# Differential scores over stacked halves, and wide matmuls for the neighbourhood heads' q and k

## The chip, the core and the metric

The kernel runs on one core of a Trainium2 chip, as one launch. The metric is the device time of a launch in microseconds (us), from start to end; lower is better. The engines named below are PE (matrix), ACT (scalar), DVE (vector), POOL (GpSimd) and SP, whose queue issues the transfers. Each works through its own list of instructions in order, and they wait for each other by semaphores.

## The reference

Two layers of an encoder over 256 tokens of width 2048, all in float32. What matters here, shortened:

```python
h = rmsnorm(x, attn_norm[l])
qd, kd, vd, qn, kn, vn = split(h @ w_in[l])        # six blocks of 1024 columns
qd, kd = rope(qd), rope(kd)                        # 8 heads x 2 maps x 64
# differential heads (8, v of 128 columns)
p = softmax(q @ k.T * 64**-0.5)                    # one for each of the two maps
o = rmsnorm((p[0] - lam * p[1]) @ v, subln_g) * (1 - lambda_init)
# neighbourhood heads (8, of 128 columns), a window in the 64-wide grid
p = softmax(q @ k.T * 128**-0.5 + bias)
o_na = rmsnorm(p @ v over all heads, na_norm[l])
x = x + concat(o, o_na) @ w_out[l]
u = relu(rmsnorm(x, mlp_norm[l]) @ w_mlp_in[l])    # 8192 wide
x = x + (u * u) @ w_mlp_out[l]
```

## The kernel before

**Split products.** A float32 operand is cut into a high and a low part (`fp32r`), and a product is three matmuls: high by high, low by high, high by low. The weights stream from HBM as slabs of 128 x 2048 (`raw`, three buffers). For each half of a slab ACT copies the high part (`whi`, line 130) and DVE subtracts to get the low part (`wlo`, line 131), with four buffers of each, so two slabs are ready ahead.

**The shapes of a product.** `block_product` (lines 140 to 171) has the activations stationary and 512 columns of weights moving; it fills two PSUM tiles of the tag `acc`, which has four buffers. It makes the q, k and v of the differential heads, v of the neighbourhood heads, and the output products. `stationary_product` has the weights stationary: for each of 16 slices three matmuls of 256 columns (lines 180 to 182), into one `acc` tile; it makes q and k of one neighbourhood head from one slab each. `wide_product` (lines 185 to 202) does the MLP's first product: the high and low activations stand side by side, so 16 matmuls of 512 columns do two of the three parts (line 192) and 16 of 256 columns the third (line 196). Its two halves are then added: ACT copies one out of PSUM (`low`), and DVE adds the other to it (`whole`, a tile of the tag `o` with four buffers).

**A layer.** Differential heads come in two blocks of four. For a block, `to_sbuf_rope` rotates q and k, transposes them and splits them into two `qkT` tiles each. `diff_head` makes the scores of both maps, each over 64 partitions (lines 362 to 364), takes exponents on ACT, combines the two maps on DVE (`wd`), transposes `wd` (line 315), copies it on ACT (`wT`), multiplies by v (line 326), squares the result on ACT (`junk`), takes the norm on POOL (`comb`), scales on DVE (`o`, line 334, tag `o`), transposes again (line 337) and splits into `mix`. Then, twice, v for four neighbourhood heads (`vs`) and four times `na_head`: q and k, scores (lines 405 to 407), exponents, a division by the sum on DVE (line 423), transposes, the split of these into `half` tiles, and three matmuls by v (lines 429 to 431). Output product and MLP follow.

**What sets the order.** A scheduler lays out each engine's list before the run. A tile waits for a free buffer of its tag. `acc` has four: v of the neighbourhood heads holds two until it is in `vs`, and each q or k holds one until it is out of PSUM.

Of the kernel before, what the change touches and what calls it, by code (L numbers as in the profile page):

```python
# [11 lines left out]
F32 = mybir.dt.float32  # L12
F32R = mybir.dt.float32r
# [5 lines left out]
P = 128  # L19
D = 2048  # L20
S = 256
# [27 lines left out]
def body(ctx, tc, x, x_t, w, gains_in, gains_o, final_g, lam_in, rpb, ident_in, rope_in, mask_in, out):  # L49
# [120 lines left out]
                one(k, t)  # L170
        return acc

    def stationary_product(h_t):

        parts = next_slab()
        acc = ps.tile([P, S], F32, name="accu", tag="acc", bufs=4)
        for k in range(NK):
            hi, lo = parts[k // 8]
            wh, wl = hi[:, (k % 8) * P:(k % 8 + 1) * P], lo[:, (k % 8) * P:(k % 8 + 1) * P]
            nc.tensor.matmul(acc, wh, h_t[k][:, 0], start=k == 0, stop=False)  # L180
            nc.tensor.matmul(acc, wh, h_t[k][:, 1], start=False, stop=False)  # L181
            nc.tensor.matmul(acc, wl, h_t[k][:, 0], start=False, stop=k == NK - 1)  # L182
        return acc

    def wide_product(h_t):


# [62 lines left out]

    def to_sbuf_rope(acc, r, which):

        dst = [act.tile([P, 4, S], F32R, name="qkT", tag="A", bufs=12) for _ in range(2)]
        for t in range(NT):
            nat = work.tile([P, NB], F32, name="nat", tag="nat", bufs=3)
            tmp = work.tile([P, NB], F32, name="tmp", tag="tmp", bufs=2)
            a3 = acc[t].rearrange("p (g d) -> p g d", d=QKD)
            n3, t3 = nat.rearrange("p (g d) -> p g d", d=QKD), tmp.rearrange("p (g d) -> p g d", d=QKD)
            G, H2 = NB // QKD, QKD // 2
            cos, sin = rope[:, t, 2 * which, :], rope[:, t, 2 * which + 1, :]  # L260
            nc.vector.scalar_tensor_tensor(n3, a3, r[t], cos[:, None, :].to_broadcast([P, G, QKD]),
                                           op0=ALU.mult, op1=ALU.mult)
            nc.vector.scalar_tensor_tensor(t3[:, :, :H2], a3[:, :, H2:], r[t],
                                           sin[:, None, :H2].to_broadcast([P, G, H2]),
                                           op0=ALU.mult, op1=ALU.mult)
            nc.vector.scalar_tensor_tensor(t3[:, :, H2:], a3[:, :, :H2], r[t],
                                           sin[:, None, H2:].to_broadcast([P, G, H2]),
                                           op0=ALU.mult, op1=ALU.mult)
            nc.gpsimd.tensor_tensor(nat, nat, tmp, op=ALU.add)
            transpose_heads(dst, nat, t)  # L270
        return dst

    def transpose_heads(dst, nat, t):
        pt = ps.tile([P, 4, P], F32, name="tp", tag="tp", bufs=2)
        for j in range(4):
            nc.tensor.transpose(pt[:, j, :], nat[:, j * P:(j + 1) * P], ident)  # L276
        hi, lo = (part[:, :, t * P:(t + 1) * P] for part in dst)
        nc.scalar.activation(hi, pt, AF.Copy)
        nc.vector.tensor_sub(lo, pt, hi.bitcast(F32))

    def to_sbuf_v(acc, r):
        v = act.tile([P, NT, NB], F32, name="v", tag="A", bufs=12)
        for t in range(NT):
            nc.scalar.activation(v[:, t, :], acc[t], AF.Copy, scale=r[t])
        return v

    def to_sbuf_v_split(acc, r):
        v = [act.tile([P, NT, NB], F32R, name="vs", tag="A", bufs=12) for _ in range(2)]
        for t in range(NT):
            split(v[0][:, t, :], v[1][:, t, :], acc[t], r[t])  # L290
        return v
# [48 lines left out]
    def split_mix(src, gain):  # L340
        m, mix_half[0] = mix_half[0], None
        i = 1
        if m is None:
            m = act.tile([P, 2, 2, S], F32R, name="mix", tag="A", bufs=12)
            mix_half[0] = m
            i = 0
        split(m[:, i, 0], m[:, i, 1], src, gain)
        return m[:, i]
# [3 lines left out]
    def diff_head(q, k, v, j, nlam, gsub):  # L352
        neg = small.tile([P, 2, NT], F32, name="neg")
        sm = small.tile([P, 2, NT], F32, name="sm")
        pr = []
        sc = [ps.tile([P, NT, S], F32, name="sc", tag="sc", bufs=2) for _ in range(2)]
        for t in range(NT):
            for m in range(2):
                rows = slice(m * QKD, (m + 1) * QKD)
                qh, ql = (part[rows, j, t * P:(t + 1) * P] for part in q)  # L360
                kh, kl = (part[rows, j, :] for part in k)
                nc.tensor.matmul(sc[m][:, t, :], qh, kh, start=True, stop=False)  # L362
                nc.tensor.matmul(sc[m][:, t, :], ql, kh, start=False, stop=False)  # L363
                nc.tensor.matmul(sc[m][:, t, :], qh, kl, start=False, stop=True)  # L364
        for m in range(2):
            nc.vector.tensor_reduce(neg[:, m, :], sc[m], axis=AX.X, op=ALU.max, negate=True)
            p = work.tile([P, NT, S], F32, name="pr", tag="pr", bufs=3)
            for t in range(NT):
                nc.scalar.activation(p[:, t, :], sc[m][:, t, :], AF.Exp, bias=neg[:, m, t:t + 1],
                                     accum_out=sm[:, m, t:t + 1])  # L370
            pr.append(p)
        rs = small.tile([P, 2, NT], F32, name="rs")
        nc.vector.reciprocal(rs, sm)
        c = small.tile([P, NT], F32, name="c")
        nc.vector.scalar_tensor_tensor(c, sm[:, 0, :], nlam, rs[:, 1, :], op0=ALU.mult, op1=ALU.mult)
        wd = work.tile([P, NT, S], F32, name="wd", tag="wd")
        for t in range(NT):
            nc.vector.scalar_tensor_tensor(wd[:, t, :], pr[1][:, t, :], c[:, t:t + 1], pr[0][:, t, :],
                                           op0=ALU.mult, op1=ALU.add)
        po = weights_times_v(wd, v, j)  # L380
        ss = small.tile([P, NT], F32, name="sso")
        for t in range(NT):
            junk = work.tile([P, HD], F32, name="junk", tag="junk", bufs=1)
            nc.scalar.activation(junk, po[:, t, :], AF.Square, scale=rs[:, 0, t:t + 1],
                                 accum_out=ss[:, t:t + 1])
        r = rms_scale(ss, NT, HD)
        comb = small.tile([P, NT], F32, name="comb")
        nc.gpsimd.tensor_tensor(comb, r, rs[:, 0, :], op=ALU.mult)
        return to_mix(po, comb, gsub)

    def na_head(h, h_t, v, rq, rb, table, gain, sq_sum):
        q = split_plain(stationary_product(h_t), [P, S], "half", 8)
        acc = stationary_product(h_t)
        kr = work.tile([P, S], F32, name="kr", tag="nat", bufs=3)
        nc.vector.tensor_mul(kr, acc, rb)
        k = split_plain(kr, [P, S], "half", 8)
        bias = work.tile([P, 6, GRID_W], F32, name="bias", tag="bias")
        th = table[:, h, :]
# [21 lines left out]
        rs = small.tile([P, NT], F32, name="rs")  # L420
        nc.vector.reciprocal(rs, sm)
        for t in range(NT):
            nc.vector.tensor_scalar(pr[:, t, :], pr[:, t, :], rs[:, t:t + 1], None, op0=ALU.mult)
        wt = split_plain(transposed_weights(pr), [P, NT, S], "wT", 3)
        po = ps.tile([P, S], F32, name="tp", tag="tp", bufs=2)
        j = h % 4
# [23 lines left out]

    def prologue(s):

        st = act.tile([P, 4, S], F32, name="xT", tag="A", bufs=12)

        def load(k0, k1):
            stream(st[:, k0:k1], x_t[s, :, k0:k1])
            for k in range(k0, k1):
                norm.store(4 * s + k, st[:, k, :])

        if s == 0:  # L460
            load(0, 2)
            x_rest[0] = lambda: load(2, 4)
        else:
            load(0, 4)

    for l in range(DEPTH):
# [62 lines left out]
        h_t = norm.h_t  # L529
        last = l == DEPTH - 1  # L530
        if last:
            gb = [act.tile([P, HALF], F32, name="gb", tag="A", bufs=12) for _ in range(2)]
            for i, g in enumerate(gb):
                nc.scalar.dma_start(g, bass.AP(tensor=final_g.tensor, offset=final_g.offset + i * HALF,
                                               ap=[[0, P], [1, HALF]]))
            xg = []
        nxt = Norm(2 * l + 2) if not last else Norm(0)
        for c in range(N_CHUNK):
            us = []
            for f in range(F_PER_CHUNK):  # L540
                u = wide_product(h_t)
                u2 = work.tile([P, S], F32, name="u2", tag="o", bufs=4)
                nc.vector.scalar_tensor_tensor(u2, u, 0.0, u, op0=ALU.max, op1=ALU.mult)
                if f % 2 == 0:
                    pair = act.tile([P, 2, 2, S], F32R, name="u2T", tag="A", bufs=12)
                split(pair[:, f % 2, 0], pair[:, f % 2, 1], u2, 1.0)
                us.append(pair[:, f % 2])
            for n in range(4):
# [113 lines left out]
```

## Time and profile before

| What | Value |
|---|---|
| device time, median of 3 runs | 2237.27 us (2236.66 to 2237.89) |
| device time of the profiled execution | 2237.57 us |
| its span, first to last instruction | 2235.7 us |
| PE busy | 2220.2 us (99%) |
| DVE busy | 1349.1 us (60%) |
| ACT busy | 1076.5 us (48%) |
| PE clock, mean granted share | 0.999 |

Matmuls are pipelined, and a new one starts before the last has ended. So what a matmul costs is the distance from its start to the next start, and not its own duration; this distance is read in the timelines.

### The profile page before, as it was taken

What the parts mean: (1) busy time and instruction counts of PE and PEld (TensorE: products, weight loads), DVE (VectorE), ACT (ScalarE), POOL (GpSimd) and SP (SyncE); (2) the same over time, 40 slices, a digit from 0 to 9 for tenths busy, and PEclk for the clock granted to TensorE, in tenths of its full rate; (3) what the DMA queues carried; (4) which work ended last, traced back from release to release, by engine and by line L of the source; (5) the groups of instructions that cost most, each with busy time, mean ns of one, the idle gap of its engine ahead of it and who ended that gap; (6) DMA issues with size and microseconds to landing.
All of it is one profiled execution on the core that took longest, in us unless ns stands there. A gap on an engine that the chain in (4) does not pass through costs nothing.

```text
span 2235.7 us, 29767 instructions
## 1 busy us (share of the span) xinstructions
PE 2220.2 (99%) x11856; PEld 1910.4 (85%) x11856; DVE 1349.1 (60%) x1743; ACT 1076.5 (48%) x1579; POOL 91.6 (4%) x136
## 2 busy tenths in 40 slices
PE   8999999999999999999999999999999999999998
PEld 7889998888888888888888899988888888888886
DVE  6657665664565565565566566666655655655654
ACT  6546544554453454454445564445434534544543
POOL 1111000000000000000010111000000000000000
PEclk9999999999999999999999999999999999999999
DMA  9443445555555555555654434554555555555553
GB/s 329 151 181 140 170 161 180 187 188 190 198 191 193 188 189 188 198 188 186 200 186 164 171 136 170 188 187 177 186 200 192 189 188 193 190 192 197 188 188 132
DMA packets 61291, 414.38 MB, mean 185 GB/s; under 512 B 7008, under 2 KB 9184, under 8 KB 11872
## 3 DMA queue, kind: packets, MB, share of 16 engines
q1 hardware_dynamic: 60720, 411.40, 51.4%
q8 instruction: 93, 1.52, 0.3%
q10 hardware_dynamic: 432, 1.08, 0.1%
q14 instruction: 46, 0.38, 0.0%
HBM read 410.35 MB, written 2.10 MB: 184 GB/s over the span
## 4 chain that ended last, share of the span: by engine, by line
PE 99%; DMA 1%; DVE 0%; ACT 0%; POOL 0%; issue 0%; ACTq 0%; POOLq 0%
PE accw L192 21%; PE acc L155 18%; PE acc L153 18%; PE acc L154 18%; PE accw L196 11%; PE accu L180 3%; PE accu L182 3%; PE accu L181 3%; PE tp L326 1%; PE tp L315 1%; PE tp L240 0%; DMA raw<-in_w 0%; PE sc L362 0%; PE tp L276 0%; PE sc L364 0%; PE sc L363 0%
## 5 line engine op out<-in xcount | busy, mean ns | idle before, releaser
L131 DVE TENSOR_TENSOR wlo<-raw,whi 128x1024 fp32r<-128x1024 f32 (+1 forms) x770 | 934.7, 1228 | 632.3 <-ACT whi L130 504.7
L130 ACT ACTIVATE whi<-raw 128x1024 fp32r<-128x1024 f32 (+1 forms) x770 | 814.2, 1058 | 905.1 <-PE acc L154 565.2
L192 PE MATMUL accw<-hT,whi 128*128 128x512 f32 x2048 | 491.2, 391 | 0.0
L192 PEld LDWEIGHTS accw<-hT,whi 128*128 128x128 f32 x2048 | 376.1, 188 | 72.8
L154 PE MATMUL acc<-whi,u2T 128*128 128x512 f32 x1024 | 399.0, 390 | 0.0
L153 PE MATMUL acc<-whi,u2T 128*128 128x512 f32 x1024 | 398.6, 389 | 0.0
L155 PE MATMUL acc<-wlo,u2T 128*128 128x512 f32 x1024 | 398.3, 389 | 0.0
L196 PEld LDWEIGHTS accw<-hT,wlo 128*128 128x128 f32 x2048 | 262.8, 191 | 10.0
L196 PE MATMUL accw<-hT,wlo 128*128 128x256 f32 x2048 | 266.0, 283 | 0.0
L153 PEld LDWEIGHTS acc<-whi,u2T 128*128 128x128 f32 x1024 | 192.2, 188 | 39.8
L155 PEld LDWEIGHTS acc<-wlo,u2T 128*128 128x128 f32 x1024 | 192.2, 188 | 39.6
L154 PEld LDWEIGHTS acc<-whi,u2T 128*128 128x128 f32 x1024 | 192.2, 188 | 39.5
L153 PE MATMUL acc<-whi,hT 128*128 128x512 f32 x512 | 202.7, 396 | 6.3 <-ACT whi L130 6.3
L154 PE MATMUL acc<-whi,hT 128*128 128x512 f32 x512 | 203.0, 396 | 0.0
L155 PE MATMUL acc<-wlo,hT 128*128 128x512 f32 x512 | 199.1, 394 | 0.1
L180 PE MATMUL accu<-hT,whi 128*128 128x256 f32 x512 | 145.6, 284 | 0.0
L181 PE MATMUL accu<-hT,whi 128*128 128x256 f32 x512 | 145.6, 284 | 0.0
L182 PE MATMUL accu<-hT,wlo 128*128 128x256 f32 x512 | 145.1, 283 | 0.0
L137 DVE SCALAR_TENSOR_TENSOR u2T<-u,u2T 128x256 fp32r<-128x256 f32 x128 | 54.4, 425 | 122.7 <-ACT u2T L136 122.7
L153 PEld LDWEIGHTS acc<-whi,hT 128*128 128x128 f32 x512 | 96.7, 189 | 27.5 <-ACT whi L130 7.4
L155 PEld LDWEIGHTS acc<-wlo,hT 128*128 128x128 f32 x512 | 96.6, 189 | 20.3 <-DVE wlo L131 0.5
L154 PEld LDWEIGHTS acc<-whi,hT 128*128 128x128 f32 x512 | 96.8, 189 | 19.6
(122 smaller groups left out, 1829.1 us busy)
## 6 DMA issues: line engine op xcount, KB each, us to landing
raw<-in_w SPq DMA_DIRECT2D x383, 1024.0 KB, 4.8
x<-in_x SPq DMA_DIRECT2D x2, 1024.0 KB, 9.7
out<-xg SPq DMA_DIRECT2D x8, 256.0 KB, 3.2
table<-in_rpb SPq DMA_DIRECT2D x4, 438.0 KB, 11.9
xT<-in_x_t SPq DMA_DIRECT2D x3, 512.0 KB, 10.2
raw<-in_w SPq DMA_DIRECT2D x4, 256.0 KB, 6.1
gb<-in_final_g ACTq DMA_DIRECT2D x2, 512.0 KB, 5.4
xT<-in_x_t SPq DMA_DIRECT2D x2, 256.0 KB, 3.9
```

The lines of the kernel that those rows point to most:

```text
L130: nc.scalar.activation(hi[:, c:c + step], r, AF.Copy)
L131: nc.vector.tensor_sub(lo[:, c:c + step], r, hi[:, c:c + step].bitcast(F32))
L137: nc.vector.scalar_tensor_tensor(dst_lo, src, scale, dst_hi.bitcast(F32), op0=ALU.mult, op1=ALU.subtract)
L153: nc.tensor.matmul(acc[t], ah, wh, start=k == 0, stop=False)
L154: nc.tensor.matmul(acc[t], al, wh, start=False, stop=False)
L155: nc.tensor.matmul(acc[t], ah, wl, start=False, stop=k == n_k - 1)
L180: nc.tensor.matmul(acc, wh, h_t[k][:, 0], start=k == 0, stop=False)
L181: nc.tensor.matmul(acc, wh, h_t[k][:, 1], start=False, stop=False)
L182: nc.tensor.matmul(acc, wl, h_t[k][:, 0], start=False, stop=k == NK - 1)
L192: nc.tensor.matmul(acc, hi[:, (k % 8) * P:(k % 8 + 1) * P], h_t[k].rearrange("p a b -> p (a b)"), start=k == 0, stop=False)
L196: nc.tensor.matmul(acc[:, :S], lo[:, (k % 8) * P:(k % 8 + 1) * P], h_t[k][:, 0], start=False, stop=k == NK - 1)
L315: nc.tensor.transpose(pw[:, kt, t * P:(t + 1) * P], pr[:, t, kt * P:(kt + 1) * P], ident)
```

## The change

The scores of the differential heads put both parts of q into the two halves of the partitions of one tile (the high part in a map's own 64 partitions, the low part in the other 64), and k's high part into both halves of a second tile; a third holds k's low part twice. Two matmuls over 128 partitions then give what three over 64 gave. The tiles are made by more, smaller instructions on ACT and DVE: for each 128 tokens two and two for q, four and four for k, where there was one and one. `na_head` takes q and k from `wide_product`, and `stationary_product` is gone. The division by the sum moves from DVE to ACT. The tag `A` has 13 buffers where it had 12. The diff, without the other lines in which only 12 becomes 13:

```diff
-    def stationary_product(h_t):
-
-        parts = next_slab()
-        acc = ps.tile([P, S], F32, name="accu", tag="acc", bufs=4)
-        for k in range(NK):
-            hi, lo = parts[k // 8]
-            wh, wl = hi[:, (k % 8) * P:(k % 8 + 1) * P], lo[:, (k % 8) * P:(k % 8 + 1) * P]
-            nc.tensor.matmul(acc, wh, h_t[k][:, 0], start=k == 0, stop=False)
-            nc.tensor.matmul(acc, wh, h_t[k][:, 1], start=False, stop=False)
-            nc.tensor.matmul(acc, wl, h_t[k][:, 0], start=False, stop=k == NK - 1)
-        return acc
-
...
-        dst = [act.tile([P, 4, S], F32R, name="qkT", tag="A", bufs=12) for _ in range(2)]
+
+
+        n_dst = 2 if which == 0 else 4
+        dst = [act.tile([P, 4, S], F32R, name="qkT", tag="A", bufs=13) for _ in range(n_dst)]
...
-            transpose_heads(dst, nat, t)
+            pt = ps.tile([P, 4, P], F32, name="tp", tag="tp", bufs=2)
+            for j in range(4):
+                nc.tensor.transpose(pt[:, j, :], nat[:, j * P:(j + 1) * P], ident)
+            ts = slice(t * P, (t + 1) * P)
+            for m in range(2):
+                own, other = (slice(i * QKD, (i + 1) * QKD) for i in (m, 1 - m))
+                hi = dst[m]
+                nc.scalar.activation(hi[own, :, ts], pt[own], AF.Copy)
+                if which == 0:
+                    nc.vector.tensor_sub(hi[other, :, ts], pt[own], hi[own, :, ts].bitcast(F32))
+                else:
+                    lo = dst[2 + m]
+                    nc.scalar.activation(hi[other, :, ts], pt[own], AF.Copy)
+                    nc.vector.tensor_sub(lo[own, :, ts], pt[own], hi[own, :, ts].bitcast(F32))
+                    nc.vector.tensor_sub(lo[other, :, ts], pt[own], hi[own, :, ts].bitcast(F32))
...
-                rows = slice(m * QKD, (m + 1) * QKD)
-                qh, ql = (part[rows, j, t * P:(t + 1) * P] for part in q)
-                kh, kl = (part[rows, j, :] for part in k)
-                nc.tensor.matmul(sc[m][:, t, :], qh, kh, start=True, stop=False)
-                nc.tensor.matmul(sc[m][:, t, :], ql, kh, start=False, stop=False)
-                nc.tensor.matmul(sc[m][:, t, :], qh, kl, start=False, stop=True)
+                both = q[m][:, j, t * P:(t + 1) * P]
+                nc.tensor.matmul(sc[m][:, t, :], both, k[m][:, j, :], start=True, stop=False)
+                nc.tensor.matmul(sc[m][:, t, :], both, k[2 + m][:, j, :], start=False, stop=True)
...
-        q = split_plain(stationary_product(h_t), [P, S], "half", 8)
-        acc = stationary_product(h_t)
+        q = split_plain(wide_product(h_t), [P, S], "half", 8)
         kr = work.tile([P, S], F32, name="kr", tag="nat", bufs=3)
-        nc.vector.tensor_mul(kr, acc, rb)
+        nc.vector.tensor_mul(kr, wide_product(h_t), rb)
...
-            nc.vector.tensor_scalar(pr[:, t, :], pr[:, t, :], rs[:, t:t + 1], None, op0=ALU.mult)
+            nc.scalar.activation(pr[:, t, :], pr[:, t, :], AF.Copy, scale=rs[:, t:t + 1])
```

**PE, where the last differential heads meet the first neighbourhood heads (first layer).** In the lists below a name's number tells one buffer's use from another; in the changed kernel line 334 is the transpose of `o`, 312 that of `wd`, 323 the product by v, 180 and 184 the wide product. Before, with heads' steps set between matmuls of q and k (`accu`):

```order
L182 MATMUL accu_1882<-hT_199,wlo_1879 128x256
L180 MATMUL accu_1882<-hT_202,whi_1878 128x256
L337 MATMUL tp_1534<-ident_75,o_1531 128x128
L181 MATMUL accu_1882<-hT_202,whi_1878 128x256
L337 MATMUL tp_1534<-ident_75,o_1531 128x128
L315 MATMUL tp_1570<-ident_75,wd_1567 128x128 x4
L182 MATMUL accu_1882<-hT_202,wlo_1879 128x256
L180 MATMUL accu_1882<-hT_205,whi_1878 128x256
```

Now, at the same heads (the second layer's list has the same rows there):

```order
L184 MATMUL accw_1875<-hT_253,wlo_1872 128x256
L184 MATMUL accw_1875<-hT_256,wlo_1872 128x256
L334 MATMUL tp_1546<-ident_75,o_1543 128x128 x2
L312 MATMUL tp_1578<-ident_75,wd_1575 128x128 x4
L323 MATMUL tp_1585<-v_1431,wT_1583 128x128 x4
L334 MATMUL tp_1604<-ident_75,o_1601 128x128 x2
L312 MATMUL tp_1637<-ident_75,wd_1634 128x128 x4
L180 MATMUL accw_1969<-hT_95,whi_1961 128x512
```

Five steps of three heads, which stood apart with matmuls of a slab between them, now stand one behind the other, ahead of the third wide product (`accw_1969`). The product by v, `tp_1527`, stands seven `L184` rows ahead of the first of them.

**DVE, at the same place.** Before (`half` is the split of q or k straight out of PSUM, `o`, `mix` and `vs` as above):

```order
L334 TENSOR_SCALAR o_1531<-tp_1515,comb_1529 128x128 x2
L131 TENSOR_TENSOR wlo_1986<-raw_1979,whi_1985 128x1024
L296 TENSOR_TENSOR half_1869<-accu_1819,half_1868 128x256
L131 TENSOR_TENSOR wlo_2045<-raw_2042,whi_2044 128x1024
L137 SCALAR_TENSOR_TENSOR mix_1474<-tp_1534,gsub_82,mix_1474 128x256
L395 TENSOR_TENSOR kr_1931<-accu_1882,rb_544 128x256
```

Now:

```order
L331 TENSOR_SCALAR o_1543<-tp_1527,comb_1541 128x128 x2
L137 SCALAR_TENSOR_TENSOR mix_1490<-tp_1546,gsub_82,mix_1490 128x256
L331 TENSOR_SCALAR o_1601<-tp_1585,comb_1599 128x128 x2
L137 SCALAR_TENSOR_TENSOR mix_1607<-tp_1604,gsub_82,mix_1607 128x256
L137 SCALAR_TENSOR_TENSOR vs_1808<-acc_1669,r_473,vs_1807 128x512
L137 SCALAR_TENSOR_TENSOR vs_1808<-acc_1670,r_479,vs_1807 128x512
L131 TENSOR_TENSOR wlo_2109<-raw_2106,whi_2108 128x1024
L131 TENSOR_TENSOR wlo_2113<-raw_2106,whi_2112 128x1024
L331 TENSOR_SCALAR o_1660<-tp_1644,comb_1658 128x128 x2
L189 TENSOR_TENSOR whole_1858<-accw_1823,low_1856 128x256
L189 TENSOR_TENSOR whole_1910<-accw_1875,low_1908 128x256
```

What empties the PSUM tiles of the first q and k moved from between the heads' steps to behind the `o` of the last head: `whole` has the tag `o` too, and the list gives its buffers out in the order of the program. At this point the four `acc` tiles are `acc_1669`, `acc_1670`, `accw_1823` and `accw_1875`.

**PE, in the second group of neighbourhood heads.** Now (line 312 transposes the probabilities, 422 to 424 multiply by v):

```order
L312 MATMUL tp_2671<-ident_75,pr_2663 128x128 x4
L422 MATMUL tp_2680<-half_2676,vs_2539 128x256
L423 MATMUL tp_2680<-half_2676,vs_2540 128x256
L424 MATMUL tp_2680<-half_2677,vs_2539 128x256
L422 MATMUL tp_2680<-half_2676,vs_2539 128x256
L423 MATMUL tp_2680<-half_2676,vs_2540 128x256
L424 MATMUL tp_2680<-half_2677,vs_2539 128x256
L180 MATMUL accw_2998<-hT_95,whi_2990 128x512
```

`half_2676` and `half_2677` are made from `tp_2671`, the row ahead. Before, the same head's transposes (`tp_2787`, line 315) and its product (`tp_2796`, line 429) stood like this, with 31 rows between them:

```order
L180 MATMUL accu_2990<-hT_95,whi_2982 128x256
L315 MATMUL tp_2787<-ident_75,pr_2779 128x128 x4
L181 MATMUL accu_2990<-hT_95,whi_2982 128x256
...
L182 MATMUL accu_2990<-hT_202,wlo_2987 128x256
L429 MATMUL tp_2796<-half_2792,vs_2631 128x256
L430 MATMUL tp_2796<-half_2792,vs_2632 128x256
```

Now two heads of each layer have no row between.

## Rows read from the trace of the kernel before

Times are in us from the start of the span, if not marked ns. A timeline row has the start, the duration, the engine, the line, the instruction (out<-in, partitions x elements) and, in brackets, idle time of the engine before it and what ended it.

**Rows 1.** The page: busy time by engine, and the chain that ended last.

```profile
PE 2220.2 (99%) x11856; PEld 1910.4 (85%) x11856; DVE 1349.1 (60%) x1743; ACT 1076.5 (48%) x1579; POOL 91.6 (4%) x136
...
PE 99%; DMA 1%; DVE 0%; ACT 0%; POOL 0%; issue 0%; ACTq 0%; POOLq 0%
```

**Rows 2.** Waits of the matrix engine: total us, times, longest us.

```profile
PE acc L153 <- ACT whi L130: 6.3, 2, 5.8
```

**Rows 3.** Groups by line, ACT: busy us, mean ns, idle before, and its releasers.

```profile
L130 ACT ACTIVATE whi<-raw 128x1024 fp32r<-128x1024 f32 x766 | 811.7, 1061 | 903.8 <-PE acc L154 565.2 <-PE accw L192 232.3 <-PE accu L181 58.1
```

**Rows 4.** The chain in order of time, MLP: start, us, what.

```profile
454.45 1.91 PE accw L196 x16
456.36 3.65 PE accw L192 x16
```

**Rows 5.** Timeline of PE, a stationary slab: start, us, instruction; 31 rows between.

```profile
208.06 0.28 PE L180 MATMUL accu<-hT,whi 128*128 128x256 f32 x1
...
211.90 0.28 PE L182 MATMUL accu<-hT,wlo 128*128 128x256 f32 x1
```

**Rows 6.** Timeline of PE, twelve score matmuls in one burst.

```profile
77.06 0.39 PE L155 MATMUL acc<-wlo,hT 128*128 128x512 f32 x1
77.38 0.39 PE L362 MATMUL sc<-qkT 64*128 64x256 f32 x2
...
78.87 0.40 PE L155 MATMUL acc<-wlo,hT 128*128 128x512 f32 x1
```

**Rows 7.** Timeline of PE, the next head: six score matmuls of one map.

```profile
84.13 0.39 PE L154 MATMUL acc<-whi,hT 128*128 128x512 f32 x1
84.45 0.38 PE L362 MATMUL sc<-qkT 64*128 64x256 f32 x1
...
85.69 0.40 PE L153 MATMUL acc<-whi,hT 128*128 128x512 f32 x1
```

**Rows 8.** Timelines of PE, ACT and DVE: weights times v to the scaled output.

```profile
200.90 1.05 PE L326 MATMUL tp<-v,wT 128*128 128x128 f32 x8
201.71 0.36 PE L181 MATMUL accu<-hT,whi 128*128 128x256 f32 x1
...
202.07 0.37 ACT L384 ACTIVATE junk<-tp,rs 128x128 f32<-128x128 f32 x1 [0.57 <-PE tp L326]
...
204.38 0.61 DVE L334 TENSOR_SCALAR o<-tp,comb 128x128 f32<-128x128 f32 x2 [1.59 <-POOL comb L388]
```

**Rows 9.** Timelines of PE, ACT and DVE: transposes, `mix`, `wT` and `vs`.

```profile
186.69 0.38 PE L337 MATMUL tp<-ident,o 128*128 128x128 f32 x2
186.90 0.60 PE L315 MATMUL tp<-ident,wd 128*128 128x128 f32 x4
187.43 0.39 PE L362 MATMUL sc<-qkT 64*128 64x256 f32 x2
...
187.10 0.47 ACT L136 ACTIVATE mix<-tp,gsub 128x256 fp32r<-128x256 f32 x1 [0.80 <-PE tp L337]
187.54 0.60 ACT L322 ACTIVATE wT<-tp 128x512 f32<-128x512 f32 x1
...
207.84 1.26 ACT L136 ACTIVATE vs<-acc,r 128x512 fp32r<-128x512 f32 x2
...
208.56 1.41 DVE L137 SCALAR_TENSOR_TENSOR vs<-acc,r,vs 128x512 fp32r<-128x512 f32 x2
```

**Rows 10.** Groups by line, ACT and DVE: the split of transposed weights.

```profile
L295 ACT ACTIVATE half<-tp 128x512 fp32r<-128x512 f32 x16 | 9.4, 588 | 9.9 <-PE tp L315 9.9
...
L296 DVE TENSOR_TENSOR half<-tp,half 128x512 fp32r<-128x512 f32 x16 | 11.0, 685 | 3.9 <-ACT half L295 3.9
```

**Rows 11.** Timeline of PE in the first microseconds, and one window after its last matmul.

```profile
9.69 0.63 PE L153 MATMUL acc<-whi,hT 128*128 128x512 f32 x1
10.12 0.63 PE L154 MATMUL acc<-whi,hT 128*128 128x512 f32 x1
...
2230.00:2231.00 1.00, 0.00 (x0) 0.00 (x0) 0.31 (x1) 0.77 (x2) 0.00 (x0) 0.50 0.56 203
```

More of the change, by code (lines that the diff above doesn't have):

```diff
@@ L269, in to_sbuf_rope @@
             nc.gpsimd.tensor_tensor(nat, nat, tmp, op=ALU.add)
-            transpose_heads(dst, nat, t)
-        return dst
[L273 to L279, printed above, removed]
+            pt = ps.tile([P, 4, P], F32, name="tp", tag="tp", bufs=2)
[13 more added lines that the diff above has]
+                    nc.vector.tensor_sub(lo[other, :, ts], pt[own], hi[own, :, ts].bitcast(F32))
+        return dst
     def to_sbuf_v(acc, r):
-        v = act.tile([P, NT, NB], F32, name="v", tag="A", bufs=12)
+        v = act.tile([P, NT, NB], F32, name="v", tag="A", bufs=13)
         for t in range(NT):
@@ L287, in to_sbuf_v_split @@
     def to_sbuf_v_split(acc, r):
-        v = [act.tile([P, NT, NB], F32R, name="vs", tag="A", bufs=12) for _ in range(2)]
+        v = [act.tile([P, NT, NB], F32R, name="vs", tag="A", bufs=13) for _ in range(2)]
         for t in range(NT):
@@ L343, in split_mix @@
         if m is None:
-            m = act.tile([P, 2, 2, S], F32R, name="mix", tag="A", bufs=12)
+            m = act.tile([P, 2, 2, S], F32R, name="mix", tag="A", bufs=13)
             mix_half[0] = m
@@ L451, in prologue @@
     def prologue(s):
-        st = act.tile([P, 4, S], F32, name="xT", tag="A", bufs=12)
+        st = act.tile([P, 4, S], F32, name="xT", tag="A", bufs=13)
         def load(k0, k1):
@@ L531, in body @@
         if last:
-            gb = [act.tile([P, HALF], F32, name="gb", tag="A", bufs=12) for _ in range(2)]
+            gb = [act.tile([P, HALF], F32, name="gb", tag="A", bufs=13) for _ in range(2)]
             for i, g in enumerate(gb):
@@ L544, in body @@
                 if f % 2 == 0:
-                    pair = act.tile([P, 2, 2, S], F32R, name="u2T", tag="A", bufs=12)
+                    pair = act.tile([P, 2, 2, S], F32R, name="u2T", tag="A", bufs=13)
                 split(pair[:, f % 2, 0], pair[:, f % 2, 1], u2, 1.0)
```

## The prediction

> **What bounds the kernel now.** The page comes first. The matrix engine is busy for 2220.2 us of a span of 2235.7, DVE for 60% and ACT for 48% of it, and the chain that ended last is PE to 99% [rows 1]. The view of waits, read next, has one entry for PE: 6.3 us at the start, for the first weights [rows 2]. So no stage has another limit: what takes PE's time away is gained, what adds to it or makes it wait is lost, and work on another engine costs something only where PE comes to wait for it. The question after that is how close the others are behind PE. The groups by line show ACT's `whi`, the first step of each slab's preparation, idle for 903.8 us ahead of its 766 instructions, and what ended the idle time is PE, giving a `whi` buffer back: 565.2, 232.3 and 58.1 us by line [rows 3]. The preparation is thus as far ahead as its buffers let it be, two slabs, in the stage of the neighbourhood heads too (the 58.1 are line 181). There is slack in the mean; what the change can spoil is order.
>
> **What the wide product gains.** In the MLP a slab takes 1.91 us for its 16 matmuls of 256 columns and 3.65 us for its 16 of 512, 5.56 together [rows 4]. A stationary slab has 48 matmuls of 256; from 208.06 to 211.90 there are 32 of them, .120 each [rows 5], so 48 take 5.76. That is .20 us gained a slab, and there are 32 (two for each of 8 heads, two layers): **6.4 us**.
>
> **What the stacked scores gain.** A differential head has 12 score matmuls over 64 partitions. Ten of the 16 heads, counted in the timeline, have them in one burst. From a product matmul at 77.06 to the one at 78.87 it is 1.81 us, and that stretch holds three product matmuls of 512 columns, worth .227 each (3.65 / 16), so the scores cost 1.81 − 3 × .227 = 1.13 us [rows 6]. In the other six heads each map has its own burst of six, and it costs 85.69 − 84.13 − 2 × .227 = 1.11 [rows 7], as much as twelve, 2.22 for the head. The rows of the first burst come in pairs that start together (x2), which rows of a lone map do not: two maps on different halves of the partitions run beside each other, one map alone does not. After the change eight matmuls over all 128 partitions follow each other at .120 [rows 5]: .96 a head, whether split or not. The gain is 10 × (1.13 − .96) + 6 × (2.22 − .96) = 1.7 + 7.6 = **9.3 us**. The Trainium skill ("TensorE: Matmul & The Clock Gate", Part 3: Packing small matmuls) states that matmuls on different row groups of the array run concurrently, and by that alone twelve would take six slots, .72 us, and stacking them would lose .24 us a head, 3.8 us in all. The trace agrees that the pairs start together, but not with that price: the burst takes 1.13, and the six split heads pay twice that.
>
> Gains: 15.7 us.
>
> **Work that is added elsewhere.** The rotation's split becomes, for each block of four heads, 8 instructions on ACT and 8 on DVE more (12 where there were 4), each on 64 partitions of 512 elements. The nearest rows are the split of transposed weights, 588 ns on ACT and 685 on DVE for 128 x 512 [rows 10]; half the partitions may cost all of that or half of it, and I take all, since a lane has the same 512 elements. That is 8 × .69 = 5.5 us of DVE in a block, over four 128-token pieces. It lies beside PE's product for v, in which a slab takes PE 48 × .120 or more, and the reserve of two slabs covers it; with the cover gone it would be 4 × 5.5 = 22 us. 32 copies and 32 additions for the wide product, and 32 scalings moved from DVE to ACT, which are no larger than the splits (under .69 us each, 22 us for 32), are far below the slack of 903.8 us. I put all of this at nothing.
>
> **New waits, where differential meets neighbourhood.** PE's list now has five steps of three heads in a row ahead of `accw_1969`, and the four `acc` tiles are all full: two hold v until `vs` has taken it, two hold the first q and k until `whole`. `vs` stands behind the `mix` of the last head but one, and `whole`, which shares the buffers of `o`, behind the last head's `o`. So PE must run down this chain before it can start the next product:
> - A: from weights times v (line 326 before) to the scaled `o`: 200.90 to 204.38 + .61 = 204.99, 4.09 us, and about .1 of hand-off (`junk` starts at 202.07, .12 after line 326 ends at 201.95) [rows 8]: 4.2.
> - B: transpose of `o`, then of the next `wd`, and its copy: from 186.69 to 187.54 + .60 = 188.14, 1.45 us, plus .1 [rows 9]: 1.55. Weights times v of that head can then start.
> - A once more: 4.2.
> - C: transpose of that `o` and `mix`: 186.69 to 187.57 on ACT [rows 9], .85 with a little left over, then `vs` on ACT .63 (1.26 for two) and on DVE .71 (1.41 for two) [rows 9], with .2 of hand-offs: 2.4.
>
> Together 12.35 us from the start of `tp_1527` to that of `accw_1969`. In it PE has work: .81 for weights times v, .81 again, two transpositions of `o` and `wd` at .74 each [rows 8, 9], and the seven matmuls of line 184 at .120: 3.94. What is left is a wait of 8.4 us. Before, the same steps were spread over products, and hid. Each layer has this once, and the second layer's list has the same rows: **16.8 us**. Behind the waiting transposes of PE stands the next slab; ACT and DVE in turn have `whi` and `wlo` of slabs to come ready early, which may queue ahead of `junk` or `o` and lengthen a link by up to 1 us.
>
> **New waits, second group of neighbourhood heads.** In two heads of each layer the product by v directly follows the transposes that it needs. From the start of the transposes it takes .60, then ACT's split .59 and DVE's .69 [rows 9, 10], with .2 of hand-offs: 2.1, of which PE fills .53 with the four transposes [rows 9]. That leaves 1.55; with a `whi` (1.06) or `wlo` sometimes in front I take 1.6, between 1.4 and 2.0. Four times: **6.4 us**.
>
> **Smaller waits** of the same sort (a `wlo` ahead of a `whole`; the output product's second pair of tiles, which waits for an addition to x) are put at 1.5, between 0 and 4.
>
> **The sum.** −6.4 − 9.3 + 16.8 + 6.4 + 1.5 = +9.0 on the profiled execution's 2237.57, which is .3 above the median of the runs: 2246.6 less .3, **2246 us**.
>
> **Rivals.** About 0.2%, 4.5 us, is what a measurement tells from no change: faster is below 2232.8, slower above 2241.7.
>
> *The waits are hidden after all, and it is faster.* The one mechanism is chain A: 204.99 − 201.95 = 3.0 us of its 4.09 pass through ACT, POOL and DVE, with 1.59 us of DVE waiting for POOL's `comb` ahead of `o` [rows 8]. That row was taken while DVE and ACT had other work; if links that ran behind other work run in a third of the time when PE stands still, 1.4 for 4.2, the first chain shrinks by 5.6 to a wait of 2.8, or 5.6 for both layers. With 2.4 for the others the sum is −15.7 + 5.6 + 2.4 = −7.7, 2230; with all hidden 2222. It decides for faster when the waits together stay under 11.2 us. Against it: the links wait for each other, which no idle engine shortens. Chance .12.
>
> *Half the waits, no change.* If `vs` or `whole` comes a head earlier than I read, one A is out of the chain, 8.4 − 4.2 = 4.2 a layer, and the sum is −15.7 + 8.4 + 6.4 + 1.5 = +.6, 2238, between 2234 and 2242. The lists on each engine speak against it, since `vs_1808` stands behind `mix_1607`. Chance .18.
>
> *The clock falls in the waits, and it is slower still.* The granted clock was 1.00 until PE's last matmul and .50 in the stretch that follows it [rows 11], so an idle PE loses it; and in the first microseconds matmuls of 512 columns stood .43 apart [rows 11] where .227 is the rule later. Some eleven of these at the start make 11 × .2 = 2.2 us for each fall. One fall in each layer, as the 8 us of waiting fall into pieces of about 3, gives 4.4: 2251, or 2250 to 2258 with the other bounds. The Trainium skill (same page, "Why this matters for your kernels") advises against idle gaps between bursts of matmuls for this reason; by that, 2251 is the likelier time. No row before has a wait in the middle of the kernel that could show it. Chance .12.
>
> **How the numbers follow.** The forecast, waits as computed, is 2242 to 2252 (smaller waits 0 to 4, links longer by up to 1 us, NA waits 1.4 to 2.0), chance .58. Faster is the first rival, .12; the same is the second, .18; slower the other two, .70. The range of 2236 to 2255 leaves out the first, .12, and pieces of the second and third, .04 each.
>
> **What would show it.** In the profile of the changed kernel: PE's waits at lines 334, 323 and 180 near the first neighbourhood heads, some 8 us a layer, ended by DVE and ACT, and at line 422 about 1.6 us in two heads of each layer; a wide slab of 5.56 us in that stage; eight scores worth .96 in every head; a granted clock of 1.00 through the waits, or a stretch below it, which would be the third rival. The prediction is wrong if chain A is much shorter than 4.2, if the rotation's extra 5.5 us shows as a wait at the scores (toward 2260 and more), or if eight stacked scores do not run at .120.

## The result and the profile after

The changed kernel takes 2256.82 us (median of 4 runs, 2256.16 to 2259.15) beside 2237.45 of the kernel before: 1.0088 of it, 95% interval 1.0076 to 1.0101, 19.4 us slower. The prediction said slower, 2246, and 2255 at most.

The profiled execution took 2259.15 us. Beside the trace of e5 below (2256.49 us, the same list of PE), some 2.0 us of its excess lie in its first 21 us, where PE waited 1.87 us for weights and the granted clock was .50 from 16.3 to 19.5. The other three runs are 2 to 3 us shorter, and stages are compared by distances inside them.

The page, busy time by engine and the chain that ended last:

```profile
PE 2220.6 (98%) x11280; PEld 1890.5 (84%) x11280; DVE 1374.9 (61%) x1775; ACT 1121.7 (50%) x1675; POOL 102.6 (5%) x136
...
PE 97%; DVE 1%; ACT 1%; DMA 1%; issue 0%; POOL 0%; ACTq 0%; POOLq 0%
```

PE has 576 instructions fewer than in [rows 1], is no less busy, and DVE and ACT now stand in the chain. The waits of PE (total us, times, longest us) name the places; before there was the one at the start [rows 2].

```profile
PE tp L334 <- DVE o L331: 11.4, 4, 2.9
...
PE tp L422 <- ACT half L292: 2.7, 4, 0.7
PE accw L180 <- DVE vs L137: 2.2, 2, 1.1
PE tp L424 <- DVE half L293: 1.6, 4, 0.5
PE tp L323 <- ACT wT L319: 1.4, 2, 0.7
PE acc L153 <- DVE whole L189: 0.6, 2, 0.3
```

These are the places that the prediction named. PE's timeline at the first of them, in the first layer (start, us, instruction, idle before it and what ended it):

```profile
195.13 1.05 PE L323 MATMUL tp<-v,wT 128*128 128x128 f32 x8
195.94 1.08 PE L184 MATMUL accw<-hT,wlo 128*128 128x256 f32 x7
199.89 0.59 PE L334 MATMUL tp<-ident,o 128*128 128x128 f32 x2 [2.88 <-DVE o L331]
200.32 0.83 PE L312 MATMUL tp<-ident,wd 128*128 128x128 f32 x4
201.84 2.07 PE L323 MATMUL tp<-v,wT 128*128 128x128 f32 x8 [0.69 <-ACT wT L319]
206.74 0.74 PE L334 MATMUL tp<-ident,o 128*128 128x128 f32 x2 [2.84 <-DVE o L331]
207.27 1.06 PE L312 MATMUL tp<-ident,wd 128*128 128x128 f32 x4
209.41 6.16 PE L180 MATMUL accw<-hT,whi 128*128 128x512 f32 x16 [1.08 <-DVE vs L137]
215.41 0.51 PE L184 MATMUL accw<-hT,wlo 128*128 128x256 f32 x3
```

From the first weights times v to `accw` it is 209.41 − 195.13 = 14.28 us, where the forecast has 12.35. The same eight matmuls of line 323 last 1.05 at first and 2.07 later, and the 16 of line 180 take 6.00 us (to 215.41) instead of 3.65 [rows 4]. The windows over this stretch tell why (us from and to, length, PE busy and instructions, granted clock, DMA share, GB/s):

```profile
196.00:200.00 4.00, 1.12 (x10) 1.00 0.13 23
200.00:204.00 4.00, 3.22 (x14) 0.57 0.58 240
204.00:208.00 4.00, 1.26 (x6) 0.50 0.00 0
208.00:210.00 2.00, 0.92 (x3) 0.50 0.00 0
210.00:214.00 4.00, 4.00 (x11) 0.50 0.00 0
214.00:218.00 4.00, 4.00 (x30) 0.98 0.02 4
```

After the first wait the granted clock falls to .50, that is 1.2 GHz, stays there through the other waits, and comes back to 2.4 GHz only when the wide product has run without a pause for a while. The second layer does the same: from the first weights times v to the end of the slab's 16 matmuls it takes 20.26 us, here 20.28. The eight stacked scores stand as forecast, with .12 from one to the next and .96 from the first to the product behind them:

```profile
79.56 0.28 PE L357 MATMUL sc<-qkT 128*128 128x256 f32 x1
79.68 0.28 PE L358 MATMUL sc<-qkT 128*128 128x256 f32 x1
...
80.52 0.40 PE L153 MATMUL acc<-whi,hT 128*128 128x512 f32 x1
```

### The profile page after: what moved, and what is told of

It reads as the page before. It is cut to its first block, busy times and chain, and to the rows that moved or that the text cites. A ratio compares the mean times of both kernels' runs of the same rounds, so it can differ in the third digit from the quotient of the medians.

```text
span 2257.3 us, 28770 instructions
## 1 busy us (share of the span) xinstructions
PE 2220.6 (98%) x11280; PEld 1890.5 (84%) x11280; DVE 1374.9 (61%) x1775; ACT 1121.7 (50%) x1675; POOL 102.6 (5%) x136
## 4 chain that ended last, share of the span: by engine, by line
PE 97%; DVE 1%; ACT 1%; DMA 1%; issue 0%; POOL 0%; ACTq 0%; POOLq 0%
PE accw L180 26%; PE acc L153 18%; PE acc L155 18%; PE acc L154 18%; PE accw L184 13%; PE tp L323 1%; PE tp L312 1%; DVE wlo L131 1%; PE tp L228 0%; DMA raw<-in_w 0%; PE sc L358 0%; PE sc L357 0%; PE tp L263 0%; PE tp L334 0%; ACT whi L130 0%
## 5 line engine op out<-in xcount | busy, mean ns | idle before, releaser
L180 PE MATMUL accw<-hT,whi 128*128 128x512 f32 x2560 | 621.6, 393 | 2.2 <-DVE vs L137 2.2
L180 PEld LDWEIGHTS accw<-hT,whi 128*128 128x128 f32 x2560 | 472.1, 189 | 94.1 <-DVE vs L137 3.0
L184 PEld LDWEIGHTS accw<-hT,wlo 128*128 128x128 f32 x2560 | 329.9, 191 | 12.3
L184 PE MATMUL accw<-hT,wlo 128*128 128x256 f32 x2560 | 337.2, 283 | 0.0
L187 ACT ACTIVATE low<-accw 128x256 f32<-128x256 f32 x160 | 60.6, 384 | 111.3 <-PE accw L184 111.3
L155 PEld LDWEIGHTS acc<-wlo,hT 128*128 128x128 f32 x512 | 96.8, 190 | 19.5 <-DVE wlo L131 0.5
L154 PE MATMUL acc<-whi,mix 128*128 128x512 f32 x256 | 100.7, 393 | 0.0
L153 PE MATMUL acc<-whi,mix 128*128 128x512 f32 x256 | 100.4, 393 | 0.0
```

The source lines that it names most:

```text
L153: nc.tensor.matmul(acc[t], ah, wh, start=k == 0, stop=False)
L154: nc.tensor.matmul(acc[t], al, wh, start=False, stop=False)
L155: nc.tensor.matmul(acc[t], ah, wl, start=False, stop=k == n_k - 1)
L180: nc.tensor.matmul(acc, hi[:, (k % 8) * P:(k % 8 + 1) * P], h_t[k].rearrange("p a b -> p (a b)"), start=k == 0, stop=False)
L184: nc.tensor.matmul(acc[:, :S], lo[:, (k % 8) * P:(k % 8 + 1) * P], h_t[k][:, 0], start=False, stop=k == NK - 1)
L187: nc.scalar.activation(low, acc[:, S:], AF.Copy)
```

## The experiments

Theory 1: the gains are as forecast, and the loss comes from the shared tag of `o` and `whole`. It orders the emptying of the `acc` tiles behind the last head's `o`, PE waits there, and the clock falls in the wait. Rival A: the wide product gives ACT and DVE too much to do, whatever the tag. Rival B: the gains are smaller than computed. Each group of experiments (e1 to e4; e5 to e8; e9 and e10) was timed beside the kernel before, on one chip.

**e1_own_tag.** The changed kernel with one line different:

```diff
-        whole = work.tile([P, S], F32, name="whole", tag="o", bufs=4)
+        whole = work.tile([P, S], F32, name="whole", tag="whole", bufs=2)
```

> The changed kernel, but `whole` has a tag of its own (two buffers) and no longer shares those of `o`. Theory 1 (order: the shared tag puts the emptying of the `acc` tiles behind the heads' `o`, and that makes the waits and the fall of the clock): in PE's list every transpose of `o` again has 26 or more rows of a product between it and the weights-times-v that it needs, and no product by v directly follows its own transposes. Then the waits of 7.5 us a layer and the four of 1.3 to 1.7 are gone, the clock stays at 1.00, and only the gains stand: 2237.5 - 15.7 + about 1 = 2223 us (2220 to 2227). Rival A (load: the wide product and the moved scaling give ACT and DVE too much to do beside the heads, whatever the tag): the waits stay, 2250 us or more. Rival B (the gains are smaller than computed): faster than before by only a few us, 2228 to 2236.

2223.98 us, 0.9939 of the kernel before (0.9926 to 0.9951). Instructions, sizes and loads are those of the changed kernel; one name is different, and 32.8 us are gone. PE's waits there, all of them:

```profile
PE acc L153 <- ACT whi L130: 6.2, 2, 6.0
PE tp L263 <- POOL nat L260: 0.4, 1, 0.4
```

Rival A falls: ACT and DVE do the same work, 50% and 62% busy, and nobody waits for it. Where the heads meet, PE's list now has matmuls of a product between weights times v and the transposes of the `o` that is made from it:

```profile
194.24 1.05 PE L323 MATMUL tp<-v,wT 128*128 128x128 f32 x8
195.04 1.08 PE L184 MATMUL accw<-hT,wlo 128*128 128x256 f32 x7
195.96 3.82 PE L180 MATMUL accw<-hT,whi 128*128 128x512 f32 x16
199.62 1.71 PE L184 MATMUL accw<-hT,wlo 128*128 128x256 f32 x13
201.17 0.38 PE L334 MATMUL tp<-ident,o 128*128 128x128 f32 x2
```

On DVE the first `whole` now stands ahead of an `o` of the differential heads. In the changed kernel it stands behind the `o` of the last of them, though ACT had copied the `low` of these two tiles at 189.76 and 197.15. First the kernel with its own tag, then the changed kernel:

```profile
197.38 0.41 DVE L189 TENSOR_TENSOR whole<-accw,low 128x256 f32<-128x256 f32 x1
198.59 0.61 DVE L331 TENSOR_SCALAR o<-tp,comb 128x128 f32<-128x128 f32 x2 [0.80 <-POOL comb L382]
```

```profile
220.71 0.61 DVE L331 TENSOR_SCALAR o<-tp,comb 128x128 f32<-128x128 f32 x2 [0.86 <-POOL comb L382]
221.24 0.74 DVE L189 TENSOR_TENSOR whole<-accw,low 128x256 f32<-128x256 f32 x2
```

**e2_scores_alone, e3_wide_alone, e4_act_scaling_alone.** One part of the change each: the first has `stationary_product` and the division on DVE back, the second and third are the kernel before with one of these:

```diff
-        q = split_plain(stationary_product(h_t), [P, S], "half", 8)
-        acc = stationary_product(h_t)
+        q = split_plain(wide_product(h_t), [P, S], "half", 8)
...
-        nc.vector.tensor_mul(kr, acc, rb)
+        nc.vector.tensor_mul(kr, wide_product(h_t), rb)
```

```diff
-            nc.vector.tensor_scalar(pr[:, t, :], pr[:, t, :], rs[:, t:t + 1], None, op0=ALU.mult)
+            nc.scalar.activation(pr[:, t, :], pr[:, t, :], AF.Copy, scale=rs[:, t:t + 1])
```

> The kernel before with only the stacked scores (and the 13 buffers); stationary products and the division on DVE stay. By the prediction's sum the scores gain 9.3 us and the rotation's extra instructions cost nothing: 2228 us. Rival B, that a part of the price of 12 matmuls over 64 partitions was the step from one tile shape to the other and comes back elsewhere: 3.9 us by the distances from start to start alone, 2233.5. Rival C, that the extra 5.5 us of DVE a block show as waits at the scores: slower than 2237.5, with a wait of PE at the score lines.

> The kernel before with only the wide product in the neighbourhood heads (`whole` still in the tag of `o`). Theory 1: the list has one bare step from weights-times-v to the transposes of `o` a layer, where the changed kernel has one bare and one with seven rows, and the four direct products by v stay. So waits of about .7 + 2.9 + 1.1 us a layer and .8 of filling the pipeline, 5.5 together, and if the clock falls 3 to 4 more: 2237.5 - 6.4 + 2 x 5.5 to 9 + 6.4 + 1 = 2249 to 2257 us. Rival (the stacked scores are part of the cause, as they alone have changed the work around that place): 2231 to 2238.

> The kernel before with only the scaling of the probabilities on ACT. Both theories: hidden, 2237.5 us, within 1. If it lies on a path that PE waits for, some us slower, with a wait of PE at the transposes of the probabilities.

The scores alone: 2228.24 us, 9.3 less than the kernel before (2237.51), as the sum had it; rival C falls, since PE waits only at the start. The scaling alone: 2237.78, ratio 1.0002 (0.9993 to 1.0010), nothing. The wide product alone: 2258.11, ratio 1.0093 (1.0079 to 1.0107), 1 us above the range expected. It alone brings the waits, so the scores are no cause of them. Its place in the first layer has one bare step less, and yet the clock is lost:

```profile
200.44 1.16 PE L326 MATMUL tp<-v,wT 128*128 128x128 f32 x8 [0.78 <-ACT wT L322]
204.43 0.73 PE L337 MATMUL tp<-ident,o 128*128 128x128 f32 x2 [2.83 <-DVE o L334]
...
207.09 5.95 PE L192 MATMUL accw<-hT,whi 128*128 128x512 f32 x16 [1.07 <-DVE vs L137]
```

**e9_wide_alone_own_tag.** The wide product alone, with the line of e1.

> The kernel before with only the wide product, and `whole` in a tag of its own: no bare step and no direct product by v in PE's list. Theory 1: nothing is left but the gain of the wide product, 32 slabs at .20 us: 2237.6 - 6.4 = 2231.2 us. If the wide product gains only what the kernel with its own tag gained beyond the scores, 13.5 - 9.3 = 4.3 us, it is 2233.3. Rival (the wide product brings waits whatever its tag): about 2258, as without the tag.

2232.93 us, ratio 0.9980 (0.9971 to 0.9989), 4.6 less than before's 2237.57. So the tag makes 25.2 us of difference in this kernel also, and the wide product gains 4.6 where 6.4 was forecast. The interval, 2.5 to 6.5 us, just reaches 6.4; e1 beside e2 gives 2228.24 − 2223.98 = 4.3, which also speaks for the smaller gain.

**e5_o_eight.** In the changed kernel, every `tag="o", bufs=4` becomes `bufs=8`.

> The changed kernel with eight buffers in the tag of `o` instead of four. Theory 1a (what counts is that `whole` and `o` share a tag and the list hands out its tiles in the order of the program, however many buffers there are): PE's list is the same, row by row at the places told of, and the time is that of the changed kernel, 2256.8 us within 1.5. Rival (a shortage: four buffers are too few for `o` and `whole` together): the waits go, and it is about 2224 as with a tag of its own.

2257.98 us (2256.49 to 2259.25), with the waits at all the new places equal to a tenth of a us (11.4, 2.7, 2.1, 1.6, 1.4, .6). It is no shortage: eight shared buffers leave the waits, while e1, with four and two, has none. As the lists read, the tag's tiles are handed out in the order of the program, with eight buffers as with four; the first `whole` still stands behind the last head's `o`:

```profile
218.35 0.61 DVE L331 TENSOR_SCALAR o<-tp,comb 128x128 f32<-128x128 f32 x2 [0.86 <-POOL comb L382]
218.88 0.75 DVE L189 TENSOR_TENSOR whole<-accw,low 128x256 f32<-128x256 f32 x2
```

**e6_first_group_own_tag, e7_second_group_own_tag.** The tag of `whole` is chosen by head (`h < 4` in e6, `h >= 4` in e7):

```diff
+        own = ("whole", 2) if h < 4 else ("o", 4)
-        q = split_plain(wide_product(h_t), [P, S], "half", 8)
+        q = split_plain(wide_product(h_t, *own), [P, S], "half", 8)
```

> The changed kernel with a tag of its own for `whole` in the first four neighbourhood heads of a layer only. PE's list then has the heads' steps spread out again, and one product by v directly behind its own transposes in each layer, where the changed kernel has two. Theory 1: 2224.0 + 2 x 1.65 + 2 x .5 for the wait at the output product = 2228 us (2226 to 2230), the clock at 1.00. Rival (the wait of 7.5 us a layer is not from these tiles): over 2245.

> The changed kernel with a tag of its own for `whole` in the last four neighbourhood heads of a layer only. The bare steps where differential heads meet neighbourhood heads stay, the direct products by v are gone. Theory 1, with 12.7 us a layer for that place, the fallen clock in it: 2224.0 + 25.4 = 2249.4 us, and about .8 for the wait at the v product behind it: 2250 (2247 to 2252). Rival (the second group's waits are the greater part): under 2240.

2229.05 and 2249.34 us. The place where differential heads meet neighbourhood heads thus costs 2249.34 − 2223.98 = 25.4 us, 12.7 a layer, and all the rest 2256.82 − 2249.34 = 7.5. Taken away in the other order, the two don't add up to the same parts: the first group's own tag saves 2256.82 − 2229.05 = 27.8 us and leaves 5.1. It changes the second group too, where PE's waits at the first of the three matmuls by v fall from 2.7 us to 1.4 (two heads where there were four).

**e8_busy_through_wait, e10_busy_24.** In the changed kernel, extra matmuls stand ahead of the transposes of `o` in two heads of each layer; nothing reads what they write (20 in e8, 24 in e10):

```diff
-        pt = ps.tile([P, S], F32, name="tp", tag="tp", bufs=2)
+        pt = ps.tile([P, 2, S], F32, name="tp", tag="tp", bufs=2)
+        for i in range(N_KEEP if keep is not None else 0):
+            nc.tensor.matmul(pt[:, 1], keep[:, 0, :P], keep[:, 0], start=True, stop=True)
```

> The changed kernel with 20 extra matmuls of 256 columns (2.4 us, into a part of the tile that nothing reads) ahead of the transposes of `o` in two heads of each layer, at the two waits of 2.9 us. The rest of the list stands as it was. They take up time in which PE is idle, so the chain of waits is as long as before. Theory 1b (half of the price of this place is the clock: 4 us a layer, 2.35 of them in the slab behind the waits, 1.0 in weights times v): the granted clock stays at 1.00 and the time falls by about 8 us to 2249 (2246 to 2252), though PE has more to do. Rival (the price is the length of the waits alone): 2257, or more where the extra matmuls run past the wait.

> As the kernel with 20 extra matmuls at two waits of each layer, with 24 (2.9 us, the whole of the wait). With 20, the first layer kept its clock of 1.00, and the second lost it in the last wait. Theory 1b: what the fall costs there is some 1.9 us in the slab behind it; if the clock now holds in both layers 2248 us (2247 to 2249.5), and if it falls in the second again 2250. Rival (the extra matmuls only delay what stands behind them): 2251 or more.

e8: 2250.01 us (ratio 1.0053, 1.0039 to 1.0066), 6.8 faster than the changed kernel, with 80 matmuls more. In the first layer the clock holds at 1.00, and the chain reads so:

```profile
193.38 1.05 PE L326 MATMUL tp<-v,wT 128*128 128x128 f32 x8
...
197.51 0.38 PE L339 MATMUL tp<-ident,o 128*128 128x128 f32 x2
...
199.01 1.16 PE L326 MATMUL tp<-v,wT 128*128 128x128 f32 x8 [0.69 <-ACT wT L322]
199.93 2.63 PE L337 MATMUL tp<-hT 128*128 128x256 f32 x20
203.00 0.59 PE L339 MATMUL tp<-ident,o 128*128 128x128 f32 x2 [0.45 <-DVE o L334]
...
205.52 3.92 PE L183 MATMUL accw<-hT,whi 128*128 128x512 f32 x16 [1.49 <-DVE vs L137]
209.28 0.52 PE L187 MATMUL accw<-hT,wlo 128*128 128x256 f32 x3
```

From weights times v to `accw` it is 205.52 − 193.38 = 12.14 us, and the slab's 16 matmuls take 3.76: 15.90 for what takes 20.28 in the changed kernel. In the second layer the chain is as short, 12.13, but right behind the last wait the granted clock falls (1.00 up to 1321, .50 from 1322 to 1324), and the slab's 16 matmuls take 5.36 us instead of 3.76. Chain and list are the same in both layers, so these 1.6 us are the clock's alone:

```profile
1308.74 1.05 PE L326 MATMUL tp<-v,wT 128*128 128x128 f32 x8
...
1320.87 5.52 PE L183 MATMUL accw<-hT,whi 128*128 128x512 f32 x16 [1.49 <-DVE vs L137]
1326.23 0.52 PE L187 MATMUL accw<-hT,wlo 128*128 128x256 f32 x3
```

e10, with four more in each wait, has 2250.85 us (2249.68 to 2252.34): it loses the clock in the second layer again, and the extra matmuls now run past the wait (12.63 us for the chain in the first layer). The rival that the price is the length of the waits alone falls with e8, though not all of e8's gain is the clock's: the chain was expected to stay as long as before, and its first A is .63 us shorter at the same clock of 1.00 (the last section has the reason), 1.3 of the 6.8 us in both layers. e10 tells the two theories apart no further. Why equal lists hold the clock in one layer and lose it in the other stays open.

## Why the prediction was right and wrong

**Right: the direction, and where.** The waits came at the lines named, in both layers, and the cause is the one read from the lists: e1, e5, e6 and e7 show it together.

**Right: the scores.** 9.3 us forecast, 9.3 measured in e2. Not all six split heads have two bursts of six: in two of them the matmuls stand as 6, 5 and 1, in two as 3 and 9. The sum does not suffer. Rival B holds only for the wide product (below). The rotation's added instructions cost 593 ns on ACT and 689 on DVE for half the partitions, all of the price of [rows 10] and not half, and are hidden. The rule of the Trainium skill on packing ("TensorE: Matmul & The Clock Gate", Part 3) would have made this part 3.8 us slower; the run decides against that price for these matmuls.

**Right: the second group.** The two heads of the first layer, from their transposes to the work behind their product:

```profile
310.32 0.80 PE L312 MATMUL tp<-ident,pr 128*128 128x128 f32 x4
...
313.16 3.80 PE L180 MATMUL accw<-hT,whi 128*128 128x512 f32 x16
...
325.00 0.60 PE L312 MATMUL tp<-ident,pr 128*128 128x128 f32 x4
...
327.90 0.39 PE L153 MATMUL acc<-whi,mix 128*128 128x512 f32 x1
```

These are 2.84 and 2.90 us, and without a wait they would be .53 + 6 × .12 = 1.25, so the heads lose 1.59 and 1.65, where 1.6 stood in the sum.

**Wrong: the term for the first place, 16.8 us.** The step that failed is "A once more" and what follows it: the links were priced at the full clock, and the fall of the clock was left to the third rival, with .12 of the chance and 2.2 us a fall. That rival is what came: one fall in each layer, and 2256.82 lies at the upper end of its 2250 to 2258. By the links, forecast and then measured in the first layer of the changed kernel: A 4.2 and 4.76, B 1.55 and 1.95, A again 4.2 and 4.90, C 2.4 and 2.67, then the slab's 16 matmuls 3.65 and 6.00. That is 16.0 against 20.28, 4.3 us a layer and 8.6 in both. With the clock held, e8 has 4.13, 1.50, 3.99, 2.52 and 3.76, 15.90 in all: chain and slab together were right to .1. The first A of the changed kernel ran at a clock of 1.00 still; its .56 is another thing (below). The other 3.7 us of the layer lie in the stretch at .50. The price of 2.2 was too low because it counted one warm-up, as at the start [rows 11], after the wait. For that part it was nearly right: the slab behind the waits took 2.35 more, and its matmuls at .50 stand .43 apart, as those at the start do. But the waits followed each other, so PE's steps between them, on which the chain hangs, ran at half the clock too: 1.37 more in B, the second A and C. The warm-up came after all of it. The Trainium skill (same page, "Why this matters for your kernels") advises against idle gaps between bursts; the trace of the changed kernel and e8 agree.

**Too large: the wide product's gain,** 4.6 for 6.4 (e9). It was taken from a slab that nothing interrupts; in this stage heads' steps stand between its matmuls. Summed from start to start over the 32 slabs, a wide one costs 5.65 us in e9's trace (5.56 forecast) and a stationary one 5.81 in the kernel before (5.76 forecast), which leaves a gain of 5.0. Of the 3.0 us by which the wide slabs are dearer, 2.6 lie in matmuls that stand next to a head's step: 512 columns behind a step take .25 to the next start, elsewhere .229. The other .4 us up to e9's 4.6 are within the noise.

The terms, forecast and measured:

| Term | Forecast | Measured | From |
|---|---|---|---|
| scores and wide product | −15.7 | −13.5 | e1 less before |
| heads meet, both layers | +16.8 | +25.4 | e7 less e1 |
| second group, smaller waits | +7.9 | +7.5 | after less e7 |
| sum | +9.0 | +19.4 | |

Of the difference of 10.4 us, 8.6 are the first place and 2.2 the gains, less .4. No other cause is needed.

## What to carry to other kernels

A tile that shares a tag with others waits for its turn in the program, and not only for a free buffer: before a new tile goes into an old tag, look in the lists for who stands ahead of it, and what PSUM it holds meanwhile. Eight buffers instead of four did not cure that; a tag of its own did, for 33 us, and made the change 13.5 us faster than the kernel before. And where PE is to wait several times in a row, price the whole stretch at the lower clock until the work behind it has run a while, not the waits alone.

## What the hardware showed unexpectedly

Extra matmuls that nobody reads, put into a wait, made the kernel 6.8 us faster (e8), by keeping the clock, through the chain in both layers and through the slab behind it in the first, and by the shorter first A.

POOL's small `v` (128 x 2) took 1.06 us in the first link A of the changed kernel and .19 in the second. In the first it ended at 198.40, as DVE's `wlo` ended at 198.35; in the second DVE stood idle:

```profile
195.76 2.59 DVE L131 TENSOR_TENSOR wlo<-raw,whi 128x1024 fp32r<-128x1024 f32 x2
```

```profile
197.34 1.06 POOL L196 TENSOR_SCALAR v<-sso 128x2 f32<-128x2 f32 x1 [9.90 <-ACT junk L378]
...
205.06 0.19 POOL L196 TENSOR_SCALAR v<-sso 128x2 f32<-128x2 f32 x1 [5.61 <-ACT junk L378]
```

In e8, where `wlo` ended before `v` began, it was .19 in both links, and the first A was 4.13 instead of 4.76. All twelve traces agree. Of their 192 `v`, 40 began while DVE worked on a `wlo`; each of these ended .05 us after that `wlo`, and took .40 to 1.07. The other 152 took .19 to .20, also those beside a `neg`, which DVE reads from PSUM. So `v` is held up until `wlo` is done. The kernel before had it already (.70 at 192.97); the prediction read A where `v` had DVE to itself. No experiment was made for this alone.
